# Expert activations of eight pairs moved into the stage that chooses experts, token sums gathered behind them

## The chip, the cores and the metric

One core of one Trainium2 chip runs the whole block in one launch. The metric is device microseconds of that core. Three timed runs of the kernel before took 2117.01, 2118.27 and 2121.99 us; the median is 2118.27 us.

## The reference

Sequence 512, width 1024, one layer. The first half is a token mixer with two kinds of attention; the change does not touch it. The second half retrieves experts by product keys:

```python
q = (xt @ w_q).reshape(t, 8, 2, 128)
sc = einsum('thpd,pkd->thpk', q, sub_keys)
top_s, top_i = top_k(sc, 16)                  # for each of two key halves
best_s, best_j = top_k(all 256 pair sums, 16) # per token and head: 16 of 16384 experts
gates = softmax(best_s)
act = gelu(xc . u_tab[ids])                   # 128 activations per token
out = sum over (head, k) of gates * act * v_tab[ids]
x = rmsnorm(x + g2 * out)
```

`u_tab` and `v_tab` hold 16384 rows of 1024 floats, 64 MB each.

## The kernel before

**Two halves of the tokens, two methods.** The 512 tokens are worked in two halves b of 256, and a half in two tiles n of 128. The first half (tiles 0 and 1) takes only the rows that it chose, each gathered by an indirect DMA that GpSimd issues, 512 KB for 128 tokens (line 816). `by_rows` (line 831) multiplies a gathered row of `u_tab` with the token's input on VectorE (line 843) and sums it to one activation; for tile 1 it later accumulates rows of `v_tab` on VectorE (line 857). `by_tokens` (line 881) does the `v_tab` side of tile 0 on TensorE: one gather and four small matmuls for a token (line 905); I call that a token sum. The second half (tiles 2 and 3) instead streams both tables whole: 128 blocks of 128 experts, two blocks a pair, 64 pairs.

**The split into two fp32r parts.** Each 512 KB unit of weights or table is loaded by SyncE's queue into one of seven buffers (tag `wraw`, which the gathers share), cast to a high part on ScalarE (line 292); the low part is a subtraction on VectorE or GpSimd (line 293, chosen from the list `low`). `mm3` (line 376) then makes three products with 24 matmuls of 256 columns.

**The stages of the second half of the tokens**, in the order of the program: the mixer; `tail(1)` with the gate and branch projections, the output projection, the transposed input `h2T`, and for each of eight heads two units of query weights, the scores and the top 16; after heads 3, 5 and 7 `choose_late` picks the experts on VectorE and ScalarE takes the exponent of the gates; then 64 steps that put the gates into a table by expert, `G0` for blocks 0 to 15 and `G1` for the rest (lines 1212 to 1233); then the 64 pairs. A pair has an s part (two units of `uT`, 48 matmuls, gelu, product with the gates, lines 1152 to 1195) and a v part (its product split in two, two units of `v_tab`, 24 matmuls of 512 columns into four accumulators, lines 1197 to 1208). The s part of pair ep+1 is written ahead of the v part of pair ep.

**What sets the order.** `by_rows` and `by_tokens` are generators. `pump` and `pump_pe` advance them at each unit, by credits of the tables `RATE` and `RATE_PE`, whose keys name the stage ("b" projections, "o1" output projection, "q1" queries, "t" a head's choice, "G" a gate step, "c" a unit of the experts). A scheduler then orders each engine's instructions, and each engine works its list in order. At the end `pump("")` empties what is left, and the last norms follow.

Of the kernel before, what the change touches and what calls it, by code (L numbers as in the profile page):

```python
# [22 lines left out]
P = 128  # L23
# [14 lines left out]
RATE = {"w": 2.2, "a": 0.75, "b": 0.5, "o1": 0.5, "q1": 0.6, "q0": 0, "r0": 0.5, "o0": 0, "c": 0.77}  # L38

RATE_PE = {"b": 0.6, "o1": 0.5, "q1": 0.75, "t": 1.5, "G": 1.1}  # L40
# [17 lines left out]
LATE = (3, 5, 7)  # L58

# [28 lines left out]
def block(ctx, tc, x, cT, w_ada, bT, b_row, g1T, norm2_g, w_in, w_pa, w_pb, w_out, lq1, lk1, lq2, lk2,  # L88
# [742 lines left out]
    def by_rows(ids, gates):  # L831
# [3 lines left out]
        for n in range(2):  # L835
            for s in range(P):
                r = next(rows)
                if s == 0:
                    h2_of[n] = h2_row(n)
                    act[n] = sb.tile([P, P], F32, name=f"act{n}")  # L840
                elif n not in h2_of:
                    h2_of[n] = h2_late(n)
                nc.vector.scalar_tensor_tensor(r, r, 1.0, h2_of[n], op0=ALU.mult, op1=ALU.mult,  # L843
                                               accum_out=act[n][:, s:s + 1])
                if s < P - 1:
                    yield
            nc.scalar.activation(act[n], act[n], AF.Gelu_apprx_tanh)
            nc.vector.tensor_mul(act[n], act[n], gates[n])
            done.append(n)
            yield  # L850
# [24 lines left out]
    def strips():  # L875
        if "z" not in part:
            part["z"] = part["home"]()
            nc.gpsimd.memset(part["z"], 0.0)
        return part["z"]

    def by_tokens():

        while 0 not in done:
            next(running[0])
        f = fr.tile([P, 256], F32, name="idf", tag="rep", bufs=4)[:, 0:P]
        nc.vector.tensor_copy(f, ids[0])
        for src, dst in ((f, ids[0]), (act[0], act[0])):
            pt = tp_ps()  # L890
            nc.tensor.transpose(pt[:, 0:P], src, ident)
            nc.vector.tensor_copy(dst, pt[:, 0:P])
        rows = ahead([(v_tab, ids[0], t) for t in range(P)])
        for t in range(P):
            r, i = next(rows), t % 32
            if t % 16 == 0 or "z" not in part:
                z = strips()
                m = 16 - i % 16
                nc.scalar.copy(z[:, 33 * i:min(33 * (i + m), D):33], act[0][:, t:t + m])
# [9 lines left out]
            if t < P - 1:  # L909
                yield  # L910
# [14 lines left out]
    def tail(b, oa, ob, finish, after):  # L925
# [96 lines left out]
        low[:] = [nc.gpsimd]  # L1022
# [6 lines left out]
        for h in range(8):  # L1029
# [12 lines left out]
            after(h)  # L1042
# [21 lines left out]
    def sums_ps(g):  # L1064
        if ga is None:
            return o_ps()[:, 0:256]
        if not late_sums:
            late_sums.append(ga.tile([P, D], F32, name="ga1", tag="ga"))
        return late_sums[0][:, 512 * (g % 2):512 * (g % 2) + 256]

    def late_psum():
        nonlocal ga
        sums_close()
# [5 lines left out]
    ga, late_guard, late_sums = None, [], []  # L1079
# [27 lines left out]

    def choose_late(h):
# [22 lines left out]
    on_pe.append(by_tokens())  # L1131
    part["home"] = lambda: wp.tile([P, D], F32, name="strips", tag="h0")
    h2d, _ = tail(1, oa, ob, finish, choose_late)
# [25 lines left out]
    h2_of.pop(1)  # L1159
    part.pop("z", None)  # L1160
    part["home"] = lambda: sb.tile([P, D], F32, name="strips", tag="ga", bufs=1)
    G0 = wp.tile([P, 2 * EARLY, 256], F32, name="G0", tag="h0")
# [25 lines left out]
    def pair(ep):  # L1188
        return experts(2 * ep, 2).rearrange("p a t -> p (a t)")
# [22 lines left out]
    for t0 in range(0, 256, 4):  # L1212
# [17 lines left out]
        nc.scalar.copy(G0[:, :, t0:t0 + 4], pv[:, 0:2 * EARLY, :])  # L1230
# [8 lines left out]
    pump_pe("")  # L1239
    w = s_part(0)  # L1240
    for ep in range(N_TILES // 2):
        nxt = s_part(ep + 1) if ep + 1 < N_TILES // 2 else None
        v_part(ep, w)
        if ep == EARLY - 1:
            more.append(wp.tile([P, 4, 1024], F32R, name="more", tag="h0"))
        w = nxt
# [43 lines left out]
```

## Time and profile before

| | us |
|---|---|
| median of three timed runs | 2118.27 |
| the profiled execution | 2120.48 |
| its span, first to last instruction | 2118.5 |
| projections and output projection of the second half | 895 to 1087 |
| queries and choice of experts | 1087 to 1228 |
| gates to the table | 1228 to 1355 |
| last token sums and a norm | 1355 to 1376 |
| 64 expert pairs | 1376 to 2103 |

Over the span TensorE is busy for 87%, VectorE 81%, GpSimd 56%, ScalarE 44%. These shares average over stages with different limits, so the table by stage below is the one to read. A window's row gives each engine's busy time with the count of its records, the clock granted to TensorE as a share of full speed, the busy share of the DMA engines and the rate. A token sum leaves eight matmul records, a row on VectorE two.

### The profile page before, as it was taken

What the parts mean: (1) busy time and instruction counts of PE and PEld (TensorE: products, weight loads), DVE (VectorE), ACT (ScalarE), POOL (GpSimd) and SP (SyncE); (2) the same over time, 40 slices, a digit from 0 to 9 for tenths busy, and PEclk for the clock granted to TensorE, in tenths of its full rate; (3) what the DMA queues carried; (4) which work ended last, traced back from release to release, by engine and by line L of the source; (5) the groups of instructions that cost most, each with busy time, mean ns of one, the idle gap of its engine ahead of it and who ended that gap; (6) DMA issues with size and microseconds to landing.
All of it is one profiled execution on the core that took longest, in us unless ns stands there. A gap on an engine that the chain in (4) does not pass through costs nothing.

```text
span 2118.5 us, 35989 instructions
## 1 busy us (share of the span) xinstructions
PE 1853.5 (87%) x13126; PEld 1649.0 (78%) x13126; DVE 1719.2 (81%) x3514; ACT 937.8 (44%) x1656; POOL 1183.4 (56%) x778
## 2 busy tenths in 40 slices
PE   6989989987788798879966578599999999999996
PEld 6889879987577686669864356389999999999995
DVE  7746775679999987976658988488988898888987
ACT  2545566442233356554331156444444444444443
POOL 2323223456767666736666557456666666666663
PEclk9999999998789999899977789799999999999998
DMA  9968675758978998969867758799999999999996
GB/s 296 273 205 250 191 202 167 215 179 264 287 262 293 305 327 296 304 195 325 286 192 239 237 182 300 279 333 337 338 332 343 335 332 335 331 331 335 334 339 226
DMA packets 370977, 589.66 MB, mean 278 GB/s; under 512 B 25278, under 2 KB 261830, under 8 KB 370800
## 3 DMA queue, kind: packets, MB, share of 16 engines
q1 hardware_dynamic: 296784, 318.37, 46.3%
q0 software_dynamic: 73728, 268.47, 36.1%
q8 instruction: 103, 1.69, 0.3%
q14 instruction: 74, 0.61, 0.1%
q10 hardware_dynamic: 288, 0.52, 0.1%
HBM read 576.18 MB, written 11.10 MB: 277 GB/s over the span
## 4 chain that ended last, share of the span: by engine, by line
PE 53%; DVE 24%; DMA 11%; issue 6%; ACT 3%; POOL 2%; SPq 1%; DVEq 0%; POOLq 0%; ACTq 0%
PE s_ps L382 16%; PE acc L1207 16%; PE mm L382 14%; DVE grow L843 7%; DMA grow<-in_v_tab_dram,ids 3%; PE g_ps L1228 2%; DVE wacc L212 2%; DMA grow<-in_u_tab_dram,ids 2%; DVE wl_k L293 1%; DMA wa<-in_w_ada_dram 1%; PE ga L905 1%; POOL grow L816 1%; DMA w_wql<-in_w_q_dram 1%; DVE oh L721 1%; PE sc L512 1%
## 5 line engine op out<-in xcount | busy, mean ns | idle before, releaser
L816 POOL DMA_INDIRECT grow<-in_u_tab_dram,ids x256 | 331.9, 1297 | 278.1 <-DVE grow L843 92.2
L816 POOL DMA_INDIRECT grow<-in_v_tab_dram,ids x256 | 292.6, 1143 | 230.0 <-DVE ga L857 94.6
L843 DVE SCALAR_TENSOR_TENSOR grow<-grow,h 128x1024 f32<-128x1024 f32 x184 | 262.5, 1434 | 29.9 <-DMA grow<-in_u_tab_dram,ids 26.4
L292 ACT CAST ehi<-eraw 128x1024 fp32r<-128x1024 f32 x145 | 151.9, 1050 | 108.5 <-PE s_ps L382 35.8
L857 DVE SCALAR_TENSOR_TENSOR ga<-grow,act,ga 128x1024 f32<-128x1024 f32 x127 | 162.5, 1280 | 11.7 <-DMA grow<-in_v_tab_dram,ids 11.3
L382 PEld LDWEIGHTS s_ps<-h2T,more 128*128 128x128 f32 x1320 | 166.8, 191 | 5.1
L382 PE MATMUL s_ps<-h2T,ehi 128*128 128x256 f32 x1168 | 154.7, 286 | 17.8 <-ACT ehi L292 17.7
L382 PE MATMUL s_ps<-h2T,more 128*128 128x256 f32 x1320 | 168.3, 283 | 0.0
L293 DVE TENSOR_TENSOR elo<-eraw,ehi 128x1024 fp32r<-128x1024 f32 x97 | 145.5, 1502 | 24.3 <-ACT ehi L292 23.3
L1207 PE MATMUL acc<-more,w 128*128 128x512 f32 x672 | 163.0, 390 | 1.6 <-DVE w L293 0.9
L382 PEld LDWEIGHTS s_ps<-h2T,ehi 128*128 128x128 f32 x1168 | 147.9, 194 | 19.7 <-ACT ehi L292 19.1
L1207 PEld LDWEIGHTS acc<-more,w 128*128 128x128 f32 x672 | 125.6, 188 | 28.1 <-DVE w L293 1.3
L1207 PE MATMUL acc<-ehi,w 128*128 128x512 f32 x576 | 145.7, 392 | 0.0
L292 ACT CAST more<-eraw 128x1024 fp32r<-128x1024 f32 x111 | 116.1, 1049 | 62.6 <-PE acc L1207 24.7
L293 POOL TENSOR_TENSOR elo<-eraw,ehi 128x1024 fp32r<-128x1024 f32 x48 | 116.4, 2424 | 12.2 <-ACT ehi L292 9.9
L293 DVE TENSOR_TENSOR more<-eraw,more 128x1024 fp32r<-128x1024 f32 x74 | 108.3, 1466 | 14.0 <-ACT more L292 13.7
L1207 PEld LDWEIGHTS acc<-ehi,w 128*128 128x128 f32 x576 | 104.2, 189 | 18.8
L382 PE MATMUL mm<-wh_v,h 128*128 128x256 f32 x640 | 103.9, 315 | 17.0 <-ACT wh_v L292 15.5
L382 PEld LDWEIGHTS mm<-wh_v,h 128*128 128x128 f32 x640 | 93.2, 216 | 22.4 <-ACT wh_v L292 18.2
L382 PE MATMUL mm<-h,wh_k 128*128 128x256 f32 x640 | 97.4, 306 | 11.0 <-ACT wh_k L292 8.9
L382 PEld LDWEIGHTS mm<-h,wh_k 128*128 128x128 f32 x640 | 87.4, 206 | 17.2 <-ACT wh_k L292 12.0
L212 DVE SCALAR_TENSOR_TENSOR wacc<-wa,cs,wacc 128x256 f32<-128x256 f32 x154 | 93.0, 625 | 8.3 <-DMA wa<-in_w_ada_dram 6.7
(315 smaller groups left out, 4569.0 us busy)
## 6 DMA issues: line engine op xcount, KB each, us to landing
eraw<-in_uT_dram SPq DMA_DIRECT2D x128, 512.0 KB
eraw<-in_v_tab_dram SPq DMA_DIRECT2D x128, 512.0 KB
wa<-in_w_ada_dram SPq DMA_DIRECT2D x48, 512.0 KB
w_v<-in_w_in_dram SPq DMA_DIRECT2D x40, 512.0 KB
w_k<-in_w_in_dram SPq DMA_DIRECT2D x40, 512.0 KB
w_gl<-in_w_in_dram SPq DMA_DIRECT2D x32, 512.0 KB
w_wql<-in_w_q_dram SPq DMA_DIRECT2D x32, 512.0 KB
w_q<-in_w_in_dram SPq DMA_DIRECT2D x24, 512.0 KB
```

The lines of the kernel that those rows point to most:

```text
L212: nc.vector.scalar_tensor_tensor(acc, wa[:, k, :], c, acc, op0=ALU.mult, op1=ALU.add)
L292: nc.scalar.copy(hi, src)
L293: (eng or nc.vector).tensor_sub(lo, src, hi.bitcast(F32))
L382: r = nc.tensor.matmul(out_ps, a(i, k), b(j, k), start=(n == 0), stop=(n == 3 * kt - 1))
L512: nc.tensor.matmul(pS[:, at[g] - o:at[g] - o + w[g]], q[g][:, s, n * P:(n + 1) * P], k3[g][:, first[g] * P:(gn + 1) * P], start=True, stop ...
L721: nc.vector.tensor_add(ohs[:, :, 0:m], ohs[:, :, 0:m], ohs[:, :, m:2 * m])
L816: nc.gpsimd.indirect_dma_start(out=r, out_offset=None, in_=tab, in_offset=bass.IndirectOffsetOnAxis(ap=ids[:, s:s + 1], axis=0))
L843: nc.vector.scalar_tensor_tensor(r, r, 1.0, h2_of[n], op0=ALU.mult, op1=ALU.mult, accum_out=act[n][:, s:s + 1])
L857: nc.vector.scalar_tensor_tensor(acc, r, a, acc, op0=ALU.mult, op1=ALU.add)
L905: nc.tensor.matmul(part["acc"][32 * q:32 * q + 32, :], z[:, 32 * i:32 * i + 32], r[:, 256 * q:256 * q + 256], start=first, stop=True, skip ...
L1207: nc.tensor.matmul(acc[b][hf], w[i][:, 256 * j + P * b:256 * j + P * b + P], V[jj][:, hf, :], start=(e == 0 and i + jj == 0), stop=(e == N ...
L1228: last = nc.tensor.matmul(pt[:, t * P:(t + 1) * P], o2[:, t, :], o1[:, t, :], start=True, stop=True)
```

## The change

The s parts of pairs 0 to 7 leave the expert stage. `first_experts`, called for each head of `tail(1)` right after its scores, loads the two units of pair h, multiplies them with `h2T` and writes the gelu into `G0`. The gate steps then multiply the gates into `G0` on VectorE where ScalarE copied them. In the expert stage pairs 0 to 7 have a v part only.

`by_tokens` starts after the output projection and no longer in the projections; the rows of `by_rows` that ran with the queries run with the projections instead. The tables change for that, and after the gates the program finishes the token sums (`while "acc" in part`) and no longer everything that is left.

```diff
-RATE = {"w": 2.2, "a": 0.75, "b": 0.5, "o1": 0.5, "q1": 0.6, "q0": 0, "r0": 0.5, "o0": 0, "c": 0.77}
+RATE = {"w": 2.2, "a": 0.75, "b": 1.6, "o1": 1.25, "q1": 0, "q0": 0, "r0": 0.5, "o0": 0, "c": 0.72}
-RATE_PE = {"b": 0.6, "o1": 0.5, "q1": 0.75, "t": 1.5, "G": 1.1}
+RATE_PE = {"q1": 1.2, "t": 1.2, "G": 1.2}
...
+                if n == 1 and s == 8:
+                    by_token()
...
-        low[:] = [nc.gpsimd]
+        low[:] = [nc.gpsimd, nc.vector] if b else [nc.gpsimd]
...
             scores(2 * b, h, qts, held)
-            after(h)
+            if b:
+                if h < EARLY:
+                    first_experts(h, h2T)
+                choose_late(h)
+            else:
+                after(h)
...
     def late_psum():
+        h2_of.pop(1)
+        G0 = wp.tile([P, 2 * EARLY, 256], F32, name="G0", tag="h0")
+        on_pe.append(by_tokens())
...
+    def first_experts(ep, h2T):
+        S = mm_ps()
+        for j in range(2):
+            U = load_unit(uT[2 * ep + j].rearrange("p (a b) -> p a b", a=KD), "u")
+            mm3(S[:, 256 * j:256 * j + 256], lambda i, k: U[i][:, k, :], lambda i, k: h2T[i][:, k, :], KD)
+        nc.scalar.activation(G0[:, 2 * ep:2 * ep + 2, :].rearrange("p a t -> p (a t)"), S, AF.Gelu_apprx_tanh)
...
-        nc.scalar.copy(G0[:, :, t0:t0 + 4], pv[:, 0:2 * EARLY, :])
+        nc.vector.tensor_mul(G0[:, :, t0:t0 + 4], pv[:, 0:2 * EARLY, :], G0[:, :, t0:t0 + 4])
...
-    pump_pe("")
-    w = s_part(0)
+    while "acc" in part:
+        next(on_pe[0])
+    nxt = None
     for ep in range(N_TILES // 2):
-        nxt = s_part(ep + 1) if ep + 1 < N_TILES // 2 else None
+        w = nxt or pair(ep)
+        nxt = s_part(ep + 1) if EARLY <= ep + 1 < N_TILES // 2 else None
         v_part(ep, w)
+        if ep == FIRST_NORM:
+            pump_pe("")
```

TensorE's list in the queries, before, from head 4's first query unit on (`wh_wql` and `wl_wql` high and low parts of query weights, `ga<-grow` token sums, four matmuls each, `sc` scores; a repeat count stands at a row's end):

```order
L382 MATMUL mm<-h2T_11326,wh_wql 128x256 x16
L905 MATMUL ga_11469<-grow,strips 32x256 x12
L382 MATMUL mm<-h2T_11326,wl_wql 128x256 x8
L905 MATMUL ga_11469<-grow,strips 32x256 x4
L742 MATMUL sc<-sk_sb,qtl 128x128
L382 MATMUL mm<-h2T_11326,wh_wql 128x256 x32
```

The same engine in the change, its last head up to the first transpose behind the choice (`wh_u` and `wl_u` are units of `uT`):

```order
L384 MATMUL mm<-h2T_11307,wl_wql 128x256 x8
L744 MATMUL sc<-sk_sb,qtl 128x128
L904 MATMUL ga_11414<-grow,strips 32x256 x8
L384 MATMUL mm<-h2T_11307,wh_u 128x256 x10
L744 MATMUL sc<-sk_sb,qtl 128x128 x3
L384 MATMUL mm<-h2T_11307,wh_u 128x256 x6
L384 MATMUL mm<-h2T_11307,wl_u 128x256 x8
L904 MATMUL ga_11414<-grow,strips 32x256 x4
L384 MATMUL mm<-h2T_11307,wh_u 128x256 x16
L384 MATMUL mm<-h2T_11307,wl_u 128x256 x8
L904 MATMUL ga_11414<-grow,strips 32x256 x20
L1173 MATMUL tp<-ident,idT 128x128 x6
```

Two units of `uT` now stand behind each head's scores, those of the last head behind the last scores, with seven token sums. ScalarE's list now loads a function table ten times where it loaded one four times: the gelu of line 1117 and the exponent of line 733 alternate three times in the choice.

TensorE's list where the gates end and the experts begin, before (`g_ps` a gate step):

```order
L1228 MATMUL g_ps<-one 128x128 x8
L905 MATMUL ga_11469<-grow,strips 32x256 x12
L1228 MATMUL g_ps<-one 128x128 x4
L905 MATMUL ga_11469<-grow,strips 32x256 x20
L382 MATMUL s_ps<-h2T_11326,ehi 128x256 x16
```

And in the change:

```order
L1233 MATMUL g_ps<-one 128x128 x8
L904 MATMUL ga_11414<-grow,strips 32x256 x4
L1233 MATMUL g_ps<-one 128x128 x4
L1212 MATMUL acc_14728<-ehi,w_14732 128x512
L1212 MATMUL acc_14729<-ehi,w_14732 128x512
```

The last token sum moved from behind the last gate step to ahead of it, and the first work of the experts is a v part.

VectorE's list in the gate steps, before and then in the change (`one` a step's masks, `G_11392` is `G0`):

```order
L1218 TENSOR_TENSOR one<-iota_ps,idT 128x512
L1224 TENSOR_SCALAR one<-iota_ps,idT 128x128 x8
L1218 TENSOR_TENSOR one<-iota_ps,idT 128x512
L1224 TENSOR_SCALAR one<-iota_ps,idT 128x128 x8
```

```order
L1223 TENSOR_TENSOR one<-iota_ps,idT 128x512
L1229 TENSOR_SCALAR one<-iota_ps,idT 128x128 x4
L1235 TENSOR_TENSOR G_11392<-g_ps,G_11392 128x16x4
L1229 TENSOR_SCALAR one<-iota_ps,idT 128x128 x4
L1235 TENSOR_TENSOR G_11392<-g_ps,G_11392 128x16x4
```

A product that waits for a step's matmuls now stands among the masks, several steps behind them.

## Rows read from the trace of the kernel before

**Rows 1.** Busy time of each engine by stage, windows.
```profile
core 0: us, PE busy (x) PEld busy (x) DVE busy (x) ACT busy (x) POOL busy (x), PEclk, DMA share, GB/s
895.00:1040.00 145.00, 128.77 (x1007) 113.29 (x1007) 98.07 (x177) 71.77 (x144) 82.09 (x54) 0.96 0.84 271
1040.00:1087.00 47.00, 30.52 (x218) 27.11 (x216) 32.20 (x64) 15.26 (x34) 24.53 (x17) 0.75 0.70 232
1087.00:1204.00 117.00, 89.51 (x736) 68.42 (x736) 96.03 (x445) 24.57 (x45) 80.53 (x57) 0.83 0.72 233
1204.00:1228.00 24.00, 2.82 (x6) 1.09 (x6) 20.97 (x115) 4.62 (x13) 4.60 (x5) 0.53 0.28 98
1228.00:1355.00 127.00, 111.47 (x1076) 75.86 (x1080) 102.61 (x288) 73.81 (x193) 95.42 (x98) 0.95 0.80 278
1376.00:2101.00 725.00, 720.84 (x4599) 657.57 (x4599) 634.42 (x583) 334.74 (x389) 451.01 (x283) 1.00 0.93 333
```

**Rows 2.** Chain of waits, one expert pair: start, length, what.
```profile
1512.09 5.75 PE s_ps L382 x48
1517.84 5.47 PE acc L1207 x24
```

**Rows 3.** Timeline of the last pair: start, length, instruction, idle before.
```profile
2095.66 0.62 ACT L292 CAST w<-wg 128x512 fp32r<-128x512 f32 x1 [4.84 <-PE acc L1207]
2096.33 1.19 PE L1207 MATMUL acc<-more,w 128*128 128x512 f32 x4 [0.71 <-ACT w L292]
2097.66 0.68 DVE L293 TENSOR_TENSOR w<-wg,w 128x512 fp32r<-128x512 f32 x1
2098.39 2.11 PE L1207 MATMUL acc<-more,w 128*128 128x512 f32 x8 [0.87 <-DVE w L293]
```

**Rows 4.** Groups of TensorE instructions, 1087 to 1204: busy, mean ns.
```profile
L382 PE MATMUL mm<-h2T,wh_wql 128*128 128x256 f32 x256 | 40.1, 313 | 17.1 <-ACT wh_wql L292 11.0 <-DVE h_k L1012 6.1
L905 PE MATMUL ga<-grow,strips 128*32 128x256 f32 x288 | 25.3, 446 | 7.1 <-DMA grow<-in_v_tab_dram,ids 5.0 <-ACT strips L899 1.1 <-issue 0.9
L382 PE MATMUL mm<-h2T,wl_wql 128*128 128x256 f32 x128 | 21.0, 311 | 4.4 <-POOL wl_wql L293 4.4
L742 PE MATMUL sc<-sk_sb,qtl 128*128 128x128 f32 x64 | 10.9, 297 | 4.2 <-ACT qtl L1039 4.2
```

**Rows 5.** Windows of line 843 alone (rows of `by_rows` on VectorE).
```profile
895.00:1040.00 145.00, 31.04 (x47) 0.96 0.84 271
1087.00:1204.00 117.00, 12.46 (x12) 0.83 0.72 233
```

**Rows 6.** DMA issues, 1087 to 1204: count, KB each.
```profile
w_wql<-in_w_q_dram SPq DMA_DIRECT2D x10, 512.0 KB
grow<-in_v_tab_dram,ids POOLq DMA_INDIRECT x36
grow<-in_u_tab_dram,ids POOLq DMA_INDIRECT x7
```

**Rows 7.** Instructions of the tiles `strips` and `w_gl`: count, ns min/median/max.
```profile
L905 PE MATMUL ops<-grow,strips x144: 379/403/636, 951.1 to 1058.0; 128*32 128x256 f32 x144
...
L293 DVE TENSOR_TENSOR wl_gl<-w_gl,wh_gl x16: 1214/1224/2151, 314.1 to 1012.3; 128x1024 fp32r<-128x1024 f32 x16
```

**Rows 8.** Groups of ScalarE instructions: a table load.
```profile
L1157 ACT ACT_TABLE_LOAD x1 | 1.3, 1283 | 0.0
```

**Rows 9.** Timeline in the choice: an elementwise product-sized VectorE instruction.
```profile
1158.39 0.21 DVE L709 TENSOR_TENSOR tkt<-tkt 128x64 f32<-128x64 f32 x1
```

**Rows 10.** Timeline from the last gate step to the first expert.
```profile
1354.61 0.54 ACT L1231 COPY G<-g_ps 128x448 f32<-128x448 f32 x1
...
1358.67 1.08 PE L905 MATMUL ga<-grow,strips 128*32 128x256 f32 x8 [0.17 <-DMA grow<-in_v_tab_dram,ids]
...
1373.57 1.06 ACT L775 ACTIVATE grow<-grow 128x1024 f32<-128x1024 f32 x1 [13.38 <-DVE grow L773]
...
1374.62 1.03 ACT L292 CAST ehi<-eraw 128x1024 fp32r<-128x1024 f32 x1
...
1375.70 0.58 PE L382 MATMUL s_ps<-h2T,ehi 128*128 128x256 f32 x1 [15.95 <-ACT ehi L292]
```

**Rows 11.** Chain of waits near the end.
```profile
2085.58 9.46 DMA grow<-in_v_tab_dram,ids
```

More of the change, by code (lines that the diff above doesn't have):

```diff
@@ L58 @@
 LATE = (3, 5, 7)
+FIRST_NORM = 10
 def bucket_of(dist):
@@ L873, in sums_close, with by_token @@
                 nc.sync.dma_start(sums_dr[t0:t1, 256 * q:256 * q + 256], st[32 * q + t0 - g:32 * q + t1 - g, :])
[L875 to L886, printed above, removed]
+    def by_token():
         f = fr.tile([P, 256], F32, name="idf", tag="rep", bufs=4)[:, 0:P]
@@ L892, in by_tokens @@
             nc.vector.tensor_copy(dst, pt[:, 0:P])
+    def by_tokens():
+        z = sb.tile([P, D], F32, name="strips", tag="ga", bufs=1)
+        nc.gpsimd.memset(z, 0.0)
         rows = ahead([(v_tab, ids[0], t) for t in range(P)])
@@ L895, in by_tokens @@
             r, i = next(rows), t % 32
[L896 to L899, printed above, removed]
+            if t % 16 == 0:
+                nc.scalar.copy(z[:, 33 * i:min(33 * i + 528, D):33], act[0][:, t:t + 16])
             first = "acc" not in part
@@ L908, in by_tokens @@
                 sums_close()
-            if t < P - 1:
-                yield
+            yield
         sums = grow()
@@ L1064, in sums_ps @@
     def sums_ps(g):
-        if ga is None:
-            return o_ps()[:, 0:256]
         if not late_sums:
@@ L1071, in late_psum @@
     def late_psum():
-        nonlocal ga
-        sums_close()
+        nonlocal ga, G0
+        h2_of.pop(1)
+        G0 = wp.tile([P, 2 * EARLY, 256], F32, name="G0", tag="h0")
+        on_pe.append(by_tokens())
         ps_guard.__exit__(None, None, None)
@@ L1077, in late_psum @@
         pools.update(ps=late_guard[0].__enter__(), tp=1)
-    ga, late_guard, late_sums = None, [], []
+    ga, G0, late_guard, late_sums = None, None, [], []
     def retrieve(h):
@@ L1130, in block @@
     oa, ob, finish = mixer(1, relieve)
-    on_pe.append(by_tokens())
-    part["home"] = lambda: wp.tile([P, D], F32, name="strips", tag="h0")
-    h2d, _ = tail(1, oa, ob, finish, choose_late)
+    h2d, _ = tail(1, oa, ob, finish, None)
     def big(nm, tag, bufs, dt=F32):
@@ L1157, in activations @@
         nc.scalar.activation(dst, S, AF.Gelu_apprx_tanh)
[L1159 to L1162, printed above, removed]
     low[:] = [nc.gpsimd]
@@ L1238, in block @@
     low[:] = [nc.vector, nc.vector, nc.gpsimd]
-    pump_pe("")
-    w = s_part(0)
+    while "acc" in part:
+        next(on_pe[0])
+    nxt = None
     for ep in range(N_TILES // 2):
-        nxt = s_part(ep + 1) if ep + 1 < N_TILES // 2 else None
+        w = nxt or pair(ep)
+        nxt = s_part(ep + 1) if EARLY <= ep + 1 < N_TILES // 2 else None
         v_part(ep, w)
+        if ep == FIRST_NORM:
+            pump_pe("")
         if ep == EARLY - 1:
             more.append(wp.tile([P, 4, 1024], F32R, name="more", tag="h0"))
-        w = nxt
     pump("")
```

## The prediction

> **What bounds the kernel now.** I read the windows by stage first, since the shares of the whole span mix stages with different limits [rows 1]. In the expert stage TensorE is busy 720.8 of 725 us at a granted share of 1.00, the higher of its levels, 2.4 GHz. Then the chain of waits: there it holds nothing but s and v parts of 5.75 and 5.47 us [rows 2]. So TensorE sets the end there, and a matmul that leaves takes its whole time along. In the queries and choice (the head loop, 1087 to 1204) no engine is full: TensorE 89.5 of 117 us, VectorE 96.0, GpSimd 80.5, DMA share 0.72 with 233 GB/s, granted share 0.83. In its last 24 us, behind the last scores, TensorE works 2.8 us, because the choice runs on VectorE. In the gate steps TensorE is busy 111.5 and VectorE 102.6 of 127 us. The change carries work from a stage that is full into one where each engine has a fifth free; the question is how much of it fits.
>
> The groups of the head loop give the price of its work [rows 4]: the 16 query units cost 40.1 + 21.0 = 61.1 us, 3.82 each, where a unit of the same 24 matmuls costs 5.75/2 = 2.88 us in the expert stage; the 36 token sums cost 25.3 us, 0.70 each; the scores 10.9.
>
> **The sum, against the profiled 2120.48 us.** Last I read the timelines of the places where parts meet; they give most of the small terms.
>
> Expert stage. Eight s parts go: 8 × 5.75 = −46.0 us.
>
> What they covered comes up. A v part takes the buffers `w` and their split from the part before it, which can't be refilled until that part's matmuls are through. Today an s part stands between two v parts, except at the last pair, and there TensorE waits 0.71 us for ScalarE's high part and 0.87 for VectorE's low part, 1.58 in all [rows 3]. In the change the v parts of pairs 0 to 6 stand back to back, six such waits: +9.5. If only the first of the two stays, 6 × 0.71 = +4.3; I take the sum because the buffers are the same.
>
> The start of the expert stage. Today the last gate copy ends at 1355.15, the last token sum at 1359.75, then a norm and the cast of the first block follow, and the first expert matmul starts at 1375.70, 15.95 us after the last sum, while its block had long been loaded: the cast stands on ScalarE behind the norm's square at 1373.57, and that waits for sums which come back through DRAM [rows 10]. In the change the last sum stands ahead of the last gate step. ScalarE's order stays norm, then cast. A step takes 127/64 = 1.98 us; the head start is that plus the 4.6 us from last copy to last sum: −6.5. Bounds are 0, if the way through DRAM starts no earlier, and −12, if the first v part also no longer waits for all of that norm.
>
> The head loop gains 14 of the 16 units of `uT` (two lie behind the last scores) and 14 token sums, 50 for 36. Without idle and at the expert stage's price TensorE would need 30 × 2.88 + 50 × 0.70 + 10.9 = 86.3 + 35.0 + 10.9 = 132 us. It won't be without idle: in the projections, the same kind of code with nothing to choose, it is busy 128.8 of 145 us, 89% at a granted share of 0.96 [rows 1]. 132/0.89 = 149 is high for a loop in which the sums fill some of the gaps; 132 is the floor; I take the middle, 140: +23. At today's price of 3.82 per unit it would be 114.6 + 35.0 + 10.9 = 160. The other engines stay below 140: VectorE loses twelve rows of `by_rows`, 12.5 us [rows 5], and gains 16 low parts of 1.22 us [rows 7], 96.0 − 12.5 + 19.5 = 103. Transfers: 14 more units, 14 more gathers of `v_tab` and 7 fewer of `u_tab` [rows 6], 21 × 0.524 MB, so 233 × 117 = 27.3 MB become 38.3 MB. That takes 115 us at the expert stage's 333 GB/s, 141 at the 271 of the projections and 164 at today's 233. The middle one lies beside my 140; it is the tightest term.
>
> The last two units and seven sums, 2 × 2.88 + 7 × 0.70 = 10.7 us, lie behind the last scores in some 21 us in which TensorE idles: 0.
>
> ScalarE loads six more function tables. Such a load took 1.28 us [rows 8]; 7.7 us more on an engine that works 24.6 of 117 us. Five hide, but the one ahead of the last exponent stands on the way to the gates: +1.3. Bounds: 0 and +7.7.
>
> The Trainium skill weighs against this, in "ScalarE: Activation LUTs", sections "What ACT_TABLE_LOAD costs" and "Table sets: the hidden batching unit": activations should be batched by table set, since a switch costs the load and a drain, about 2.66 us. The trace agrees on the load and shows no drain; if all six switches were exposed at the page's figure, an estimate of 16 us from that page, my sum would end 5 us above the kernel before.
>
> Gate steps. 64 products on VectorE replace 64 ScalarE copies. An elementwise instruction of 128 × 64 with all operands in SBUF took 0.21 us in the choice [rows 9]; 64 × 0.21 = 13.4 us against 127 − 102.6 = 24.4 us in which VectorE idles. The new products wait for matmuls with masks behind them, so part shows: I take +4, between 0 and +13.4. The sums there stay 71 for 74, nothing.
>
> Projections and output projection. 18 token sums go, 18 × 0.70 = −12.6 on TensorE, and 32 rows of `by_rows` come, at 31.04/47 × 2 = 1.32 us each [rows 5] (a row leaves two records) 42 us on VectorE, which works 98.1 + 32.2 = 130 of 192 us there and would reach 172. The gathers exchange, 18 for 32. I take +3, between −12.6 and +19, which is what would show if half of the 42 us failed to fit the 62 that are idle and the sums gave back a little.
>
> The end. Two more rows stay over behind the last pair; the chain ends on a gather of 9.46 us [rows 11] and a row costs about what it does elsewhere, 1.3: +2, between 0 and +4.
>
> Sum: −46.0 + 9.5 − 6.5 + 23 + 1.3 + 4 + 3 + 2 = −9.7, so 2110.8 in a profiled execution. That one lay 2.2 us above the median of the timed runs: 2108.6, rounded to 2108.
>
> **Rivals.**
>
> *The stage takes nearly everything.* The sums fill the gaps, the loop takes its 132 us (+15 for +23), the projections give the 12.6 us of sums back, and the products cost nothing in the gate steps: −9.7 − 8 − 15.6 − 4 = −37.3, 2083.2 profiled, 2081 timed. For it: a fifth of each engine is idle there, and VectorE has 62 us free in the projections. Against: those stages have waits from engine to engine that no average shows.
>
> *The loop becomes bound by transfers: slower than before.* `w_u`, `w_wql` and the gathers share the same seven buffers, and a buffer comes free only when cast and low part, or a token's four matmuls, are done. If the rate stays at 233 GB/s, 38.3 MB take 164 us, +47 for +23: −9.7 + 24 = +14.3, 2132.6 timed. It decides from 150 us of loop on, 38.3 MB at 255 GB/s. For it: the rate today, and that gathers issue one by one on GpSimd, 80.5 us busy already, and slices with a DMA share of 0.84 reach only 271. Against: twelve row products fewer hold buffers, and half of the low parts are VectorE's now, at 1.22 us each.
>
> *VectorE bounds the gate steps: no change.* The whole 13.4 us come on top there, 9.4 more: 2118. For it: a product waits for TensorE in the middle of masks that the next step's matmuls wait for. Against: several steps of masks lie between.
>
> **How the numbers follow.** Forecast 0.45, with its own range 2100 to 2116; nearly everything fits 0.22; bound by transfers 0.18; VectorE in the gates 0.15. What a measurement of this kernel tells from no change is about 0.2%, 4.2 us: faster is below 2114.0, slower above 2122.5. Of the forecast 0.38 is faster and 0.07 the same; of the first rival all is faster, of the second all slower, of the third 0.03, 0.09 and 0.03. So 0.63, 0.16, 0.21. The range 2079 to 2132 leaves out some 0.09 of the first rival and 0.09 of the second.
>
> **What would show it.** Right: an expert stage without eight s parts, so 46 us shorter but for six gaps near 1.6 us among its first seven v parts; a head loop from 132 to 150 us with TensorE at or above 0.88 of it; VectorE above 110 of some 131 us in the gates; the first expert matmul some 14 us after the last gate step. Wrong: a head loop of 155 us and more with the DMA rate near 233 GB/s (then transfers), projections and output projection shorter than 185 us (then the sums there were on the path), gate steps over 137 us, gaps between v parts over 2 us, because gathers then collide with the blocks' loads, or a granted share in the loop still at 0.83, which would price the units near 3.8 us.

## The result, and the profile after

The changed kernel took 2205.78 us (median of four runs, 2198.36 to 2216.49) where the kernel before took 2117.64 (2110.19 to 2121.99): 1.0424 times as long, 95% interval 1.0366 to 1.0482. The profiled execution took 2210.82 us, its span is 2208.7. The forecast was 2108 with a range from 2079 to 2132: wrong in sign and far outside.

Where the 90 us between the two spans lie is read from five TensorE matmuls that begin or end a stage. The first two columns give when each starts (us); "longer by" is how much longer the stretch from the row above has become (from the span's start, for the first row):

| | before | changed | longer by | forecast |
|---|---|---|---|---|
| first query unit | 1087.4 | 1091.4 | +4.0 | +3 |
| first gate step | 1228.9 | 1274.1 | +41.2 | +24.3 |
| last gate step | 1351.5 | 1398.4 | +1.7 | +4 |
| first expert matmul | 1375.7 | 1414.8 | −7.8 | −6.5 |
| last expert matmul | 2102.8 | 2192.3 | +50.4 | −36.5 |
| end of the span | 2118.5 | 2208.7 | +0.7 | +2 |

Four of six terms came within 3 us, not all of them for the reasons given (below). The head loop cost 17 us more than forecast, and the expert stage, which was to lose 36.5 us, got 50.4 longer: 87 of the 100 us by which the sum is off lie there.

The windows of the changed kernel, which answer to [rows 1] (stages by its own borders):

```profile
895.00:1040.00 145.00, 117.71 (x873) 108.16 (x874) 135.35 (x226) 69.19 (x142) 96.48 (x63) 0.94 0.91 298
1040.00:1091.00 51.00, 32.93 (x231) 30.80 (x230) 44.21 (x85) 18.91 (x38) 31.29 (x23) 0.83 0.81 284
1091.00:1249.00 158.00, 136.59 (x1203) 109.71 (x1197) 97.68 (x443) 50.91 (x72) 84.69 (x64) 0.94 0.78 257
1249.00:1274.00 25.00, 11.22 (x93) 6.75 (x91) 20.56 (x118) 7.09 (x16) 12.95 (x12) 0.75 0.56 192
1274.00:1400.00 126.00, 113.14 (x1080) 74.86 (x1080) 110.37 (x350) 65.60 (x130) 92.70 (x95) 0.98 0.79 274
1415.00:2192.00 777.00, 714.51 (x4222) 628.87 (x4223) 540.03 (x527) 314.95 (x364) 412.11 (x255) 0.95 0.82 284
```

In the last row every engine has become less busy than in [rows 1]: TensorE 714.5 of 777 us where it was full, DMA share 0.82 for 0.93, VectorE 540 of 777. No engine became the bound: the engines wait for one another. Inside the stage, 1500 to 2050, before and then changed:

```profile
1500.00:2050.00 550.00, 550.00 (x3530) 502.80 (x3529) 483.84 (x423) 254.67 (x297) 349.30 (x218) 1.00 0.94 335
```

```profile
1500.00:2050.00 550.00, 509.94 (x3131) 455.47 (x3131) 378.03 (x358) 226.59 (x262) 298.30 (x184) 0.97 0.82 285
```

What VectorE waited for in that stretch (total, times, longest), before and then changed:

```profile
DVE ga L857 <- DMA grow<-in_v_tab_dram,ids: 7.0, 13, 1.5
DVE grow L843 <- DMA grow<-in_u_tab_dram,ids: 2.2, 2, 1.8
```

```profile
DVE ga L861 <- DMA grow<-in_v_tab_dram,ids: 119.5, 55, 5.8
DVE grow L845 <- DMA grow<-in_u_tab_dram,ids: 38.1, 15, 5.1
```

what TensorE waited for in the changed kernel (before, no such wait stands in that stretch):

```profile
PE acc L1212 <- DVE w L295: 40.0, 19, 6.0
```

and how long GpSimd's gathers waited for a low part to free a buffer, before and then changed:

```profile
POOL grow L816 <- DVE elo L293: 6.4, 2, 4.1
POOL grow L816 <- DVE more L293: 6.0, 3, 3.1
```

```profile
POOL grow L818 <- DVE more L295: 51.7, 14, 6.3
POOL grow L818 <- DVE elo L295: 40.5, 13, 5.2
```

So VectorE stands 157.6 us before rows of `by_rows` whose gathers have not landed, and what is queued behind the row, the split of `w` and low parts of expert units, makes TensorE wait; the low parts that come late hold up further gathers, 92 us for 12. One such place in the timeline (start, length, instruction, idle before):

```profile
1811.48 0.95 POOL L818 DMA_INDIRECT grow<-in_v_tab_dram,ids  x1 [2.02 <-DVE ga L861]
...
1813.85 1.29 DVE L861 SCALAR_TENSOR_TENSOR ga<-grow,act,ga 128x1024 f32<-128x1024 f32 x1 [2.63 <-DMA grow<-in_v_tab_dram,ids]
1815.04 1.22 DVE L295 TENSOR_TENSOR more<-eraw,more 128x1024 fp32r<-128x1024 f32 x1
1816.18 0.68 DVE L295 TENSOR_TENSOR w<-wg,w 128x512 fp32r<-128x512 f32 x1
...
1816.92 1.20 PE L1212 MATMUL acc<-ehi,w 128*128 128x512 f32 x4 [2.27 <-DVE w L295]
...
1818.20 1.04 ACT L294 CAST ehi<-eraw 128x1024 fp32r<-128x1024 f32 x1 [3.81 <-PE acc L1212]
1818.27 0.94 POOL L818 DMA_INDIRECT grow<-in_v_tab_dram,ids  x1 [4.60 <-PE acc L1212]
```

The row waits 2.63 us; a low part and the split of `w` wait behind it; TensorE waits 2.27; the next cast waits for TensorE and keeps its buffer; the next gather comes after 4.60 us in which GpSimd is idle. Matching the k-th gather on GpSimd with the k-th row on VectorE gives a row's lead (from the issue of its gather to its start): before, the mean is 8.9 us between 1500 and 2050, changed 6.9. A unit held its buffer 11.3 us from issue to the end of its low part before, 15.7 in the changed kernel.

The stall comes and goes. Pair lengths, worked out from ScalarE's timeline as the distance of successive gelus, from pair 8 on (before, they are 11.2 but for a few early ones):

```
11.2 11.2 11.7 13.5 12.4 11.2 12.2 11.2 17.3 11.2 11.2 11.2 17.6 11.2 11.2 11.4 11.6 11.3 15.4 12.6 12.3 19.2 11.2 12.1 16.0
```

(the 10th to the 34th of 55; mean of all 12.59 us). 28 of the 55 keep the old pace, 11.4 us or less.

### The profile page after: what moved, and what is told of

It is laid out like the page before. It is cut to its first block, busy times and chain, and to the rows that moved or that the text cites. A ratio compares the mean times of both kernels' runs of the same rounds, so it can differ in the third digit from the quotient of the medians.

```text
span 2208.7 us, 35929 instructions
## 1 busy us (share of the span) xinstructions
PE 1887.1 (85%) x13126; PEld 1662.5 (75%) x13126; DVE 1671.7 (76%) x3575; ACT 938.5 (42%) x1596; POOL 1170.4 (53%) x772
## 5 line engine op out<-in xcount | busy, mean ns | idle before, releaser
L818 POOL DMA_INDIRECT grow<-in_v_tab_dram,ids x256 | 282.3, 1103 | 314.6 <-DVE ga L861 74.2
L845 DVE SCALAR_TENSOR_TENSOR grow<-grow,h 128x1024 f32<-128x1024 f32 x207 | 288.4, 1402 | 11.9 <-DMA grow<-in_u_tab_dram,ids 9.6
L294 ACT CAST ehi<-eraw 128x1024 fp32r<-128x1024 f32 x129 | 135.5, 1050 | 242.6 <-PE acc L1212 127.2
L1212 PE MATMUL acc<-ehi,w 128*128 128x512 f32 x576 | 165.2, 422 | 74.8 <-DVE w L295 52.2
L295 POOL TENSOR_TENSOR elo<-eraw,ehi 128x1024 fp32r<-128x1024 f32 x43 | 105.2, 2446 | 26.2 <-ACT ehi L294 25.3
L384 PE MATMUL s_ps<-h2T,ehi 128*128 128x256 f32 x912 | 118.7, 283 | 0.0
L295 DVE TENSOR_TENSOR elo<-eraw,ehi 128x1024 fp32r<-128x1024 f32 x86 | 112.3, 1306 | 7.1 <-ACT ehi L294 6.3
L384 PEld LDWEIGHTS s_ps<-h2T,ehi 128*128 128x128 f32 x912 | 113.6, 192 | 0.1
L384 PE MATMUL mm<-h,wh_k 128*128 128x256 f32 x640 | 99.0, 309 | 15.7 <-ACT wh_k L294 14.2
L904 PE MATMUL ga<-grow,strips 128*32 128x256 f32 x1024 | 82.4, 398 | 27.5 <-DMA grow<-in_v_tab_dram,ids 15.9
L845 DVE SCALAR_TENSOR_TENSOR grow<-grow,h2p 128x1024 f32<-128x1024 f32 x49 | 59.4, 1217 | 60.0 <-DMA grow<-in_u_tab_dram,ids 47.3
```

What stands on the lines that cost most here:

```text
L294: nc.scalar.copy(hi, src)
L295: (eng or nc.vector).tensor_sub(lo, src, hi.bitcast(F32))
L384: r = nc.tensor.matmul(out_ps, a(i, k), b(j, k), start=(n == 0), stop=(n == 3 * kt - 1))
L818: nc.gpsimd.indirect_dma_start(out=r, out_offset=None, in_=tab, in_offset=bass.IndirectOffsetOnAxis(ap=ids[:, s:s + 1], axis=0))
L904: nc.tensor.matmul(part["acc"][32 * q:32 * q + 32, :], z[:, 32 * i:32 * i + 32], r[:, 256 * q:256 * q + 256], start=first, stop=True, skip ...
L1212: nc.tensor.matmul(acc[b][hf], w[i][:, 256 * j + P * b:256 * j + P * b + P], V[jj][:, hf, :], start=(e == 0 and i + jj == 0), stop=(e == N ...
```

## The experiments

All kernels that are not called otherwise are the changed kernel with one edit; ratios are to the kernel before.

**The rate of rows.** `RATE["c"]`, 0.77 before and 0.72 in the change, sets how many rows of `by_rows` run per expert unit.

```diff
-RATE = {... "c": 0.72}
+RATE = {... "c": 0.75}      # e1; e4 0.77
```

> The changed kernel with one number altered: the credit of an expert unit 0.75 for 0.72, so that a pair of four units always issues three rows, seven buffers in all, as many as the ring has. Theory A (the rate 0.72 makes rows and units turn against the seven buffers, so that now and then a row's gather gets its buffer only a few VectorE instructions ahead of that row, and VectorE, then TensorE, wait): the pairs run at 11.2 us as in the kernel before instead of 12.6 on the mean, the stalls of VectorE on gathers in the expert stage fall from about 150 us to under 30, and the time falls from 2206 to about 2130 us. Theory B (the eight v parts in a row leave every engine's order out of step for the rest of the stage, whatever the rate): pairs stay at 12.4 to 12.8 us, 2195 to 2210 us.

Measured 2211.85 us, 1.0471 (1.0435 to 1.0507), mean pair 12.75. The pattern that repeats evenly is as bad; theory A in this form fell.

In the kernel before, with nothing moved:

```diff
-RATE = {... "c": 0.77}
+RATE = {... "c": 0.72}
```

> The kernel before with the credit of an expert unit 0.72 for 0.77, nothing moved. Theory A: a third to a half of its pairs take over 12 us, the mean pair is 12 to 12.6 us for 11.2, so +50 to +85 us, and some 13 rows more stay over behind the last pair, +15 to +20: 2185 to 2220 us. Theory B: pairs stay at 11.2 us and only the rows left over cost: about 2135 us.

2183.06 us, 1.0331 (1.0272 to 1.0390); mean pair 11.97, at 11.2 from the tenth to about the 30th pair, then 10.9 to 18.3. From first to last expert matmul its trace takes 783.7 us for 727.1 before; some 12 us more go to rows left over behind the last pair, which the changed kernel does not have. The lower rate alone makes most of the stage's loss, without any v part in a row; theory B fell.

```diff
-                if h < EARLY:
-                    first_experts(h, h2T)
-        nc.vector.tensor_mul(G0[...], pv[...], G0[...])
+        nc.scalar.copy(G0[...], pv[...])
-        nxt = s_part(ep + 1) if EARLY <= ep + 1 < N_TILES // 2 else None
+        nxt = s_part(ep + 1) if ep + 1 < N_TILES // 2 else None      # and w = s_part(0) first
```

> The changed kernel with its s parts put back: first_experts is not called, the gates are copied into G0 by ScalarE, all 64 pairs have an s part in the expert stage; rates, token sums from the choice on and the split of low parts stay as changed (0.72). Theory A: the pairs stall as in the changed kernel, mean 12 to 12.8 us from the first pair on, so about 2170 to 2200 us, although the head loop falls from 158 to about 125 us. Theory B: with no eight v parts in a row the pairs run at 11.2 us and the time is 2105 to 2125 us.

2149.76 us, 1.0173 (1.0119 to 1.0228), mean pair 11.72: it stalls in the second half, and briefly at pairs 12 to 15. Between the two theories. From its first query unit to the first gate step it takes 132.7 us, the changed kernel 182.7: the sixteen units cost 50 us there, more than the 46 that they leave.

> The changed kernel with the expert credit of the kernel before, 0.77. In its instruction order 14 rows stand five or fewer VectorE instructions behind what frees their gather's buffer (22 at 0.72, 2 in the kernel before). Theory A: part of the stall goes, mean pair 11.6 to 12.1 us, 2150 to 2180 us. Theory B: 2195 to 2210 us. If the rate were all of it and the phase nothing: 2125 to 2135 us.

2175.66 us, 1.0296 (1.0246 to 1.0346): 30 us better than at 0.72, as theory A had it, though a pair still takes 12.40 us on the mean. In the traces 18 of the 31 us lie in the expert stage; 11 lie ahead of the first query unit, where the two programs are the same, so they are scatter.

**The lead of a gather.**

```diff
-    def ahead(order):
+    def ahead(order, LOOK=1):         # by_rows calls it with 2
```

> The changed kernel with by_rows issuing its gathers two rows ahead instead of one, rate 0.72. Theory C: it is the lead. In the kernel before, a row of the expert stage starts 8.8 us (median; 7.2 the least) after its gather was issued and rows hardly wait; in the changed kernel 7.0 us, 71 of 124 rows wait for their gather, and what is queued behind them on VectorE makes TensorE wait. With a row more of lead the waits go: pairs at 11.2 to 11.5 us for 12.6, about 2125 to 2140 us. Theory E: it is the number of buffers. A gather more in flight takes one of the seven from the units: pairs at 12.6 us or more, 2200 to 2240 us. Theory B (the eight v parts in a row put the stage out of step, rows have no part in it): 2195 to 2210 us.

2198.34 us, 1.0377 (1.0334 to 1.0420); pairs 12.43, and the lead in the trace is 6.7 us, no longer than with one ahead. Theory C fell: the gather stands earlier in the program, but it still gets its buffer when one of the seven comes free, and that sets the lead.

```diff
-RATE = {... "c": 0.72}
+RATE = {... "c": 0}
```

> The changed kernel with the credit of an expert unit 0: no row of by_rows runs beside the pairs, all 177 run behind the last one (some 230 us longer there). Theories C and E: the pairs from 8 on run at 11.2 us and TensorE does not wait on VectorE's split of w, so that the stage to the last pair is 56 x 11.2 = 627 us from the first gelu on, where it was 699. Theory B: pairs at 12 to 12.8 us without any row. In either case the six waits between back-to-back v parts of the first pairs stay, 1.5 to 2 us each, if they come from the single buffer of w.

2339.84 us in one run, and every pair from the second on takes 11.2 us. So rows are needed for the stall; the v parts in a row do not start it. Their waits are seen alone here, two of them:

```profile
1424.92 1.20 PE L1212 MATMUL acc<-ehi,w 128*128 128x512 f32 x4 [0.75 <-ACT w L294]
1426.27 1.19 PE L1212 MATMUL acc<-ehi,w 128*128 128x512 f32 x4 [0.15 <-DVE w L295]
...
1431.85 1.19 PE L1212 MATMUL acc<-ehi,w 128*128 128x512 f32 x4 [0.75 <-ACT w L294]
1434.37 1.21 PE L1212 MATMUL acc<-ehi,w 128*128 128x512 f32 x4 [1.33 <-DVE w L295]
```

0.8 to 2.1 us each, 7.7 for the six. In the changed kernel, where rows run among them, they come to 11.3; I had forecast 9.5 from [rows 3].

In the kernel before:

```diff
-LOOK = 1
+LOOK = 2
```

> The kernel before with all its gathers issued two ahead instead of one (token sums too). Theory C: its expert stage has no waits to lose, pairs stay at 11.2 us and the time within 10 us of 2112. Theory E: the seven buffers are short already at 11.2 us per pair: pairs of 11.8 us and more, 2150 us or more.

2114.63 us, 0.9989 (0.9972 to 1.0007): no change, as theory C had it and E had not.

**The head loop.**

```diff
-RATE_PE = {"q1": 1.2, "t": 1.2, "G": 1.2}
+RATE_PE = {"q1": 0.4, "t": 0, "G": 1.82}
```

> The changed kernel with its token sums taken out of the queries: 12 sums for 50 in the head loop, none at a head's choice, 115 for 71 in the gate steps (those get longer by up to 44 x 0.70 = 31 us). Transfers in the loop fall from 40.7 to about 21 MB. Theory T (the loop of 158 us is bound by transfers and their buffers): the loop falls to TensorE's 30 x 2.88 + 12 x 0.70 + 10 = 105 us or little more, 105 to 125 us. Theory V (the loop waits for the choice on VectorE and for casts behind the exponent on ScalarE): it stays over 140 us.

2204.28 us in one run. From the first query unit to the last score it takes 117 us for 157, and TensorE fills it; theory T holds. The choice then ends later, the gate steps get no longer, and the sums run behind them:

```profile
1084.00:1201.00 117.00, 110.90 (x900) 102.04 (x901) 86.48 (x368) 50.50 (x68) 51.33 (x29) 0.96 0.54 172
1201.00:1237.00 36.00, 6.35 (x36) 4.41 (x34) 33.02 (x195) 8.49 (x18) 4.22 (x4) 0.58 0.13 44
1237.00:1361.00 124.00, 114.57 (x1116) 77.14 (x1120) 110.11 (x351) 66.46 (x130) 100.31 (x103) 0.96 0.87 304
1361.00:1425.00 64.00, 40.48 (x328) 7.86 (x328) 0.92 (x2) 2.86 (x6) 36.51 (x39) 0.60 0.93 339
```

The 38 sums had cost 41 us in the loop, 1.07 each. Some 26 of these are TensorE's own time (136.6 us busy for 110.9), near the forecast 0.70 each; the other 15 are idle time of TensorE that goes with the sums and their gathers. Whether the transfers or the seven buffers held TensorE up, no run separates: in the changed loop the rate swings between 0 and 370 GB/s in slices of 4 us.

**The order of VectorE's list.** Here the four instructions of the expert stage are written as letters: r a row, L a low part of a unit (GpSimd's are not in it), W the low half of `w`, and a bar the product `wg` that ends a group. The groups of pairs 28 to 32 before and 29 to 35 in the change:

```
before   LrWLrLr | LrWLrLr | rLWLrr | LrLrWLr | LrrWLLr
changed  rrLWLrr | LLWrrL | LrWrLrL | rrLWLr | rLLWrrL | LrWrLL | rrLWLr
```

Before, rows and low parts alternate. In the change a round of three pairs repeats in which two rows, then two low parts, stand side by side. Counted in the traces, from the last gate step to the last expert matmul, two rows stand side by side 22 times before, and 48, 49, 43, 51 and 47 times in the changed kernel, e1, e4, e5 and e2; in e3, which stalls late, 36. (The expectations count in the lists as built, which gives one to four more.) At 0.80 and 0.85 the list alternates, 20 times each.

```diff
-RATE = {... "c": 0.72}
+RATE = {... "c": 0.80}      # e10: 0.85
```

> The changed kernel with the credit of an expert unit 0.80. Theory F: it is the pattern in which VectorE's list has rows and low parts. In the kernel before they alternate (24 times two rows stand next to each other in the expert stage); in the changed kernel, at rates 0.75 and 0.77 and with gathers two ahead it falls into a round of three pairs with two rows and two low parts side by side (52, 53, 46 and 53 times), and the product or split of w stands behind two gathers. At 0.80 the list alternates again (23 times): pairs 11.2 to 11.5 us, 2120 to 2140 us. Theory G (VectorE has too much to do in a pair, whatever the order): more rows per pair make it no better than at 0.77, 2175 us or more.

2129.03 us, 1.0070 (1.0036 to 1.0103), mean pair 11.28. TensorE's row in the stage, and what it and VectorE still waited for:

```profile
1500.00:2050.00 550.00, 547.84 (x3507) 499.81 (x3507) 466.60 (x417) 254.37 (x294) 354.62 (x218) 1.00 0.94 336
```

```profile
PE acc L1212 <- DVE w L295: 2.2, 2, 1.7
```

```profile
DVE ga L861 <- DMA grow<-in_v_tab_dram,ids: 47.1, 45, 3.9
DVE grow L845 <- DMA grow<-in_u_tab_dram,ids: 17.0, 8, 4.2
```

More rows per pair, and the stage is full again; rows still wait at times (64 us for 158), but TensorE hardly waits behind them (2.2 us for 40.0). Theory G fell.

> The changed kernel with a credit of 0.85, 24 times two rows side by side. Theory F: pairs 11.2 to 11.6 us while rows run and 11.2 in the last six or so, which have none; 2115 to 2140 us. Theory G: slower than 0.77, over 2180 us.

2128.59 us, 1.0069 (1.0037 to 1.0102), mean pair 11.38. As theory F had it.

```diff
-    low[:] = [nc.vector, nc.vector, nc.gpsimd]
+    low[:] = [nc.vector, nc.gpsimd]           # e11; e12 with 0.77
```

> The changed kernel at 0.72 with the low parts of the expert stage in turn on VectorE and GpSimd (it was VectorE twice, GpSimd once), which takes 0.67 low parts of 1.22 us a pair from VectorE. Two rows side by side 26 times. Theories F and G alike: pairs near 11.2 to 11.5 us, 2120 to 2145 us. If GpSimd's longer low parts (2.4 us) delay its gathers, 2150 us or more.

2227.80 us, 1.0528 (1.0454 to 1.0601): the slowest of all, mean pair 13.27, though two rows stand side by side 23 times only. The count of side-by-side rows is thus not the cause by itself. Nor did the edit relieve VectorE: between 1500 and 2050 the low parts that it kept took 2.0 us on the mean where they took 1.35, so that 83 of them cost as much as 116 (164 us for 157). One of the two groups of these low parts, in the changed kernel and then in e11:

```profile
L295 DVE TENSOR_TENSOR elo<-eraw,ehi 128x1024 fp32r<-128x1024 f32 x57 | 76.9, 1349 | 1.6 <-ACT ehi L294 1.5
```

```profile
L295 DVE TENSOR_TENSOR elo<-eraw,ehi 128x1024 fp32r<-128x1024 f32 x41 | 83.8, 2043 | 1.9 <-ACT ehi L294 1.8
```

> As the run before, low parts in turn on VectorE and GpSimd, with a credit of 0.77: two rows side by side 51 times. It has the same engine loads but for 0.2 rows a pair. Theory F: stalls come back, pairs of 11.8 to 12.6 us, 2150 to 2200 us. Theory G: as fast as the run before within 10 us.

2198.28 us, 1.0388 (1.0324 to 1.0452), mean pair 12.56: better than e11, against theory F. With two low parts of 2.4 us a pair on GpSimd other things decide too; which, no run tells.

**Gather or VectorE time.**

```diff
+            if r is None:                     # rows of v_tab from the fifth on: no gather
+                r = part["src"]               # a part of G1
```

> The changed kernel at 0.72, with the last 124 rows of by_rows (tile 1's rows of v_tab) left without gathers: they read a part of G1 in place of a gathered row, so the VectorE work stays and 124 of the 128 gathers of v_tab rows go. If a row stalls the stage by its gather (late buffer, late data): pairs at 11.2 to 11.5 us once those rows run, from about 1630 us on, where the changed kernel has 12.6. If by its time on VectorE: 12 us and more.

2157.09 us in one run. Inconclusive: rows without a gather ran early, 20 in 50 us, which fills VectorE (third number) while they last; pairs took 11.2 to 17 us until they were through, and 11.2 from then on.

```profile
1640.00:1900.00 260.00, 242.17 (x1493) 216.24 (x1492) 258.81 (x201) 108.96 (x125) 72.43 (x28) 0.97 0.51 169
```

```diff
-                nc.vector.scalar_tensor_tensor(acc, r, a, acc, op0=ALU.mult, op1=ALU.add)
+                nc.vector.scalar_tensor_tensor(acc[:, 0:64], r[:, 0:64], a, acc[:, 0:64], op0=ALU.mult, op1=ALU.add)
```

> The opposite: the same rows keep their gathers, but VectorE works 64 of their 1024 columns (the rest of tile 1's sum is left out), some 0.2 us for 1.28. If the gather is the cause: stalls stay, pairs of 12 us and more. If VectorE's time is: 11.2 to 11.5 us.

2204.47 us in one run, mean pair 12.66. With these rows nearly free the stall stays, and what VectorE saved between 1500 and 2050 (264 us busy for 378) became waiting for gathers, 279 us with rows of `u_tab` for 158:

```profile
DVE ga L861 <- DMA grow<-in_v_tab_dram,ids: 246.8, 76, 7.6
```

So the row's time on VectorE does not stall the stage. That its gather does is read from these waits and from e6; the run meant to show it, e13, did not settle it.

**One kernel, both orders.**

```diff
+        RATE["c"] = 0.85 if ep < 20 else 0.72
         nxt = s_part(ep + 1) if EARLY <= ep + 1 < N_TILES // 2 else None
```

> The changed kernel with a credit of 0.85 in pairs 0 to 19 and 0.72 from then on. VectorE's list alternates rows and low parts in the first part and falls into the round of three pairs with rows and low parts side by side some six pairs after the switch. Theory F: pairs at 11.2 us on the mean up to about pair 25, stalls with pairs of 13 to 17 us behind it, mean over 12.2 there. If the state at the stage's start decided: 11.2 us throughout. If rows of v_tab (from about pair 16 on) stalled whatever the order: stalls from pair 16 on.

2138.09 us in one run. Its list, read pair by pair, falls into the round at pair 44, not six pairs behind the switch as I wrote. The pairs take 11.2 us up to pair 43, and the first long one ends with pair 44's gelu at 1876.56. Two groups of the round's form, at pairs 41 and 42, had passed without a wait. The windows ahead of it and behind:

```profile
1500.00:1864.00 364.00, 364.00 (x2345) 333.05 (x2344) 314.45 (x276) 171.44 (x198) 230.38 (x142) 1.00 0.93 332
1864.00:2050.00 186.00, 172.84 (x1083) 154.48 (x1082) 136.30 (x115) 78.67 (x91) 103.59 (x65) 0.99 0.83 291
```

For 23 pairs at 0.72 TensorE is full; with the round comes the stall. So it is neither the rate as such, nor rows of `v_tab`, nor the stage's start. What changes there is the order; no run gave one rate two orders by hand, so this is the best account left, not a direct proof.

**What is left of the change, and a better placing.**

> The changed kernel with the s parts put back and a credit of 0.77; VectorE's list then alternates (two rows side by side 28 times), where with the s parts moved and 0.77 it does not (46). Theory F: pairs at 11.2 us; the time within 8 us of the kernel before (2116), so that the other parts of the change (token sums from the choice on, low parts in turn, rows with the projections) cost or give little, and the moved activations cost the 13 us that are left at 0.80. If the rates and sums cost the rest: 2125 us or more.

(e3's edit with 0.77.) 2128.91 us, 1.0058 (1.0035 to 1.0081). That is 5 us over what I expected, and what I had written for "the rates and sums cost the rest": without the moved activations the rest of the change is slower than before, with some pairs of 14 to 16 us in its first third, though its list alternates (27 times two rows). e9, at 0.80 with the activations moved, takes as long, so no gain of moving them shows; the two differ in their rate, too.

```diff
-                if h < EARLY:
-                    first_experts(h, h2T)
+                for ep in {0: (0,), 1: (1,), 2: (2,), 4: (3,), 6: (4,), 7: (5, 6, 7)}.get(h, ()):
+                    first_experts(ep, h2T)      # and "c": 0.80
```

> The changed kernel at 0.80 with the eight pairs spread otherwise over the heads: one each behind the scores of heads 0, 1, 2, 4 and 6, and three behind those of head 7, where TensorE is busy 11 of the 25 us to the gate steps. Four units less stand in the head loop: if that is bound by TensorE and transfers it gets 4 x 2.88 to 4 x 3.7 = 11 to 15 us shorter, and the 11.5 us of matmuls lie in the 14 idle ones behind it: 2114 to 2122 us. If the transfers only move behind the scores, too, the choice's end gets as much longer: 2127 to 2133 us.

2114.22 us, 0.9976 (0.9958 to 0.9995): the one kernel whose interval lies below the kernel before, by 0.05 to 0.42%; with so many kernels tried, that is weak. From its first query unit to the first gate step it takes 173.9 us, e9 182.5.

> The kernel at 0.80 with four pairs behind the last scores (heads 0, 1, 2 and 4 one each). If TensorE's idle time to the gate steps still holds the fourth (4 x 5.75 = 23 us and sums in some 32 us): 2105 to 2112 us, ahead of the kernel before by 0.3% or more. If the transfers of eight units (4.2 MB) behind the scores delay the gate steps: 2114 to 2122 us.

2115.61 us, 0.9998 (0.9972 to 1.0024). The last score comes 9 us earlier than in e16 (1224.3), the first gate step 1 us later (1266.4): what leaves the loop comes back behind the scores, where TensorE now works 33.5 of 41.6 us.

## Why the prediction was wrong, point by point

**The step that failed is the first term, "Eight s parts go: 8 × 5.75 = −46.0 us".** The stage from first to last expert matmul, which was to lose 36.5 us with this term and the next, gained 50.4. The subtraction is sound only if the other pairs keep their 11.22 us, and I took that for granted because TensorE was full there [rows 1, 2]; they took 12.59. The change also lowered the expert credit from 0.77 to 0.72, and the prediction gives that edit no price in the stage: fewer rows looked like less work. What I did not see is how little room the stage had on another path than TensorE's. Before, a row started 8.9 us after its gather was issued, and where a trace of a full stage gives a gather's landing its median is 7.2 or 7.3 us (e7, the kernel before with two ahead, and here e9):

```profile
grow<-in_v_tab_dram,ids POOLq DMA_INDIRECT x128, 7.3
```

The scheduler's order of VectorE's list held that path open, and both the rate (e2, e3) and the moved s parts (at 0.77 the stage stalls throughout with them moved, e4, and only in its first third without, e15) let it fall into another one. None of my rivals had it. Where the stall is gone, the stage gives back most of what was forecast, not all: 24.9 us in e9 (702.2 for 727.1), 27.8 in e16 and 32.2 in e18, for 36.5. Even then the change is no faster: in e9 the head loop takes 17 us more than its term and the stage 12, and smaller terms give back 13. 2129 us lie inside the range, near its slow end.

**Back-to-back v parts**: 11.3 us in the changed kernel, 7.7 without rows (e6), for +9.5, the mechanism as written.

**Start of the expert stage**: −7.8 for −6.5, right. TensorE's row there answers to the last of [rows 10]:

```profile
1414.84 3.78 PE L1212 MATMUL acc<-ehi,w 128*128 128x512 f32 x8 [15.26 <-ACT ehi L294]
```

**Head loop**: +41.2 to the first gate step for +24.3. TensorE's own time came out near the floor that I had put at 132: 136.6 us busy, at a granted share of 0.94. (By the reckoning of [rows 4] a unit costs 3.6 or 3.4 us here, between my 2.88 and the 3.82 of before; times of interleaved groups overlap.)

```profile
L384 PE MATMUL mm<-h2T,wh_wql 128*128 128x256 f32 x256 | 39.3, 311 | 9.1 <-ACT wh_wql L294 9.1
L384 PE MATMUL mm<-h2T,wl_wql 128*128 128x256 f32 x128 | 18.4, 285 | 1.4 <-DVE wl_wql L295 1.3
L384 PE MATMUL mm<-h2T,wh_u 128*128 128x256 f32 x236 | 33.4, 289 | 0.1
L384 PE MATMUL mm<-h2T,wl_u 128*128 128x256 f32 x112 | 15.9, 284 | 0.9 <-DVE wl_u L295 0.9
L904 PE MATMUL ga<-grow,strips 128*32 128x256 f32 x407 | 33.3, 405 | 8.3 <-DMA grow<-in_v_tab_dram,ids 6.6 <-issue 1.7
```

But that is 136.6 of 158 us, 0.86 where I had asked for 0.88. The transfers, which I called the tightest term, were 40.7 MB for my 38.3 and ran at 257 GB/s for the 271 that I leaned on: 158 us. TensorE's longest waits are for casts of query weights (9.1 us) and for gathers (6.6); those casts had stood 33.2 us before loads that had not landed. The second rival was right about the place and, with 158 us of loop for its 164, about most of the size there; e8 shows that without 38 of the sums the loop is TensorE's at 117. One reading in that rival and in the term was wrong: the "twelve rows" that VectorE loses are twelve records [rows 5], six rows; the 12.5 us stand.

**Gate steps**: +1.7 for +4. The products took 0.21 us as in [rows 9], and VectorE had room for them. The third rival fell.

**Projections**: +4.0 for +3, which is luck: over sixteen traces of kernels that are the changed one up to there, the first query unit starts anywhere from 1075.3 to 1095.5, with a median near 1085, for 1087.4 before. **End**: +0.7 for +2, but not as written: in neither kernel did a row stay over behind the last expert matmul.

**Table loads**: six more, 1.28 us each as the Trainium skill says ("ScalarE: Activation LUTs", "What ACT_TABLE_LOAD costs"); the drain that this page of the skill adds has no row here. ScalarE was busy 50.9 of 158 us in the loop, and no run took the loads away, so what they cost there is not shown.

**What stays open**: which feature of the order decides. The alternation tells the runs with the changed kernel's division of low parts (two rows side by side 13 to 27 times where the stage is fast, 36 to 51 where it stalls), but not those with more low parts on GpSimd (23, and slowest). One number does tell them all: between 1500 and 2050 a row's mean lead is 7.9 us or more in the kernels whose mean pair is under 11.4 us (before, e9, e10, e15, e16, e18) and 6.4 to 7.3 in those where it is 11.9 or more (changed, e1, e2, e4, e5, e8, e11, e12, e14); e3 and e17, between them, have 8.0 and 7.8. It is what the stall looks like, though, and not shown to be what starts it.

## What to carry to other kernels

Before work is taken out of a stage that one engine fills, find the second path that has no room there: how long a prefetched row's gather leads its use, against how long it takes to land, with the buffers that all streams share. If an instruction list is ordered by a scheduler, a changed rate of background work is a change of every order behind it, and comparing the lists pair by pair shows what a subtraction of busy times can't. And a stage whose engines are all four fifths busy has the transfers' room to check first, not TensorE's.

## What the runs showed of the hardware that I had not expected

All engines can wait together: in one kernel (e17) the stage runs with TensorE full and a DMA share of 0.93, and then at 0.83 with every engine less busy, at the same credit of 0.72. Issuing a gather earlier in the program gave no lead at all (6.7 us for 6.9), as it is the buffer's release that starts it.

VectorE's product `wg` of 0.68 us took up to 3.05 where it met a low part on GpSimd:

```profile
1819.11 3.05 DVE L1199 TENSOR_TENSOR wg<-wg,G 128x512 f32<-128x512 f32 x1
1819.23 2.37 POOL L295 TENSOR_TENSOR elo<-eraw,ehi 128x1024 fp32r<-128x1024 f32 x1
```

It ends 0.56 us behind GpSimd's instruction, as if nearly all of it ran after that one. The Trainium skill ("SBUF — State Buffer", "SBUF: two separate sides") has a port pair that the two share and that one of them locks for a whole instruction; these rows agree with it, except that the skill gives the pair to the one that starts first, and VectorE's record starts 0.12 us earlier here. This is not what stalls the changed kernel: between 1500 and 2050 VectorE's products, splits and low parts ran over half a microsecond over their time 54 times before and 25 times in the change. In e11 it is 51 times, 39 of them low parts, which is where the time went that the edit was to save; no run tested whether that alone makes it the slowest.
